# Loads moved to GpSimd's queue, and the conditions' rows read from memory, in a two-layer hybrid block

## The chip, the cores and the metric

The kernel runs on one core of a Trainium2 chip. The metric is the device time of one execution, in microseconds: before the change a median of 3194.43 us over three runs, from 3187.32 to 3200.40. The engines are named as in the profile: PE is TensorE (the matmuls), DVE VectorE, ACT ScalarE, POOL GpSimd, and SP SyncE, which only issues transfers. Each engine works through its own queue of instructions in order. ScalarE and GpSimd issue transfers too, and such an instruction stands in their queue like any other.

## What is computed

Two layers work on 1024 latent tokens `x` and 256 context tokens, each of width 1024. Every layer scales and shifts its normed input by six vectors that come from a condition, adds a mixer's output, and then an MLP's with a squared ReLU.

```python
mod_l = (silu(c) @ ada_w[l] + ada_b[l]).reshape(b, 6, 1, D)      # latent tokens
mod_c = (silu(c_ctx) @ ada_w[l] + ada_b[l]).reshape(6, D)        # context tokens
h_l = modulate(rmsnorm(x, norm1_g[l]), mod_l[:, 0], mod_l[:, 1])
x = x + mod_l[:, 2] * mixer(h_c, h_l)      # layer 0: attention and retention, layer 1: state space
h_l = modulate(rmsnorm(x, norm2_g[l]), mod_l[:, 3], mod_l[:, 4])
x = x + mod_l[:, 5] * (square(relu(h_l @ w1)) @ w2)
```

The context tokens take the same path in layer 0 with `mod_c`. The mixer of layer 1 (`s5_mixer`) runs a complex linear recurrence for 64 groups of 16 channels in both directions, and a gated output, `za * sigmoid(zb)` with `gelu(y) @ w_glu`, follows it.

## The kernel before

Tokens lie along the free axis in three blocks, 0 and 1 of 512 latent tokens and 2 of 256 context tokens; channels lie on the 128 partitions, eight tiles deep. Products in float32 are made of three matmuls (`mm3`, lines 68 to 72) from a high and a low part of each operand: L70 and L71 take the high weights, L72 the low ones, and the parts are made by `hi` (L76, mostly on ScalarE) and `lo` (L84, VectorE or GpSimd). Weights come through `split` (L1004): SP loads 512 KB into `mraw`, three buffers deep, ScalarE makes `uh` (or `dh`), VectorE `ul` (or `dl`).

The stages in order are: the first modulations, attention and retention, the output product, the first MLP in two passes (blocks 0 and 2 together, from about 1074 us, and block 1 alone, from about 1635 us), the state-space mixer (about 2085 to 2268 us), the gated output (to about 2475 us) and the second MLP.

In an MLP the hidden blocks go in pairs: a pair's first product is put through the ReLU and squared on ScalarE (`r`, L1053, `ah`, L1056), GpSimd makes its low part (`al`, L84), and the second product of the pair is added to `x` by VectorE (L1070), which frees the bank for TensorE.

Beside the first MLP side work is drawn in pieces, at a fixed rate for each matmul. It is, in order: the condition rows (`ada_row`), the modulation vectors of layer 1 (`ada_rest` with `aw` loads and a VectorE product-and-sum, L216), the tables of the state-space mixer, its input coefficients (`s5_inputs`, which loads `wb` and `ww`, L1347 and L1350, multiplies them to `wo` on VectorE, L1365 to L1369, and stores them as `bst` from ScalarE's queue), more tables (`tq`, `ta`), and the mixer's input for blocks 0 and 2 (`s5_in`, which stores `us` to `ud` in memory, L1454). Block 1's input follows after the MLP.

`ada_row` (L198 to L200) loads the condition to all partitions as `silr` from GpSimd's queue, and ScalarE puts the Silu on it. It is called at the start, ahead of the first MLP, and at the end of the state-space mixer, there for the last three modulation vectors, whose 96 `aw` loads of 128 KB are drawn during the gated output.

The mixer's loop takes 32 pairs of groups: `spread` negates and copies the oscillation table `CS` on ScalarE, `states` builds the decay `dec` on ScalarE, makes the inputs on TensorE (L1501), multiplies and scans them on VectorE (`st`, `sm`, `sz`), and makes `sy` on VectorE or GpSimd; `outs` brings these to the outputs on TensorE (L1536).

The framework orders each engine's instructions itself when the program is built, by its own estimate of when each could run. So the order in the queues is not that of the source: a change in one place can move instructions elsewhere, and one in the source may move none. [...] The pool of tiles from which `aw`, `wb`, `ww`, `wo` and others of 512 columns come (`atile`) has 32 buffers, and the one of 256 columns 16.

Of the kernel before, what the change touches and what calls it, by code (L numbers as in the profile page):

```python
# [18 lines left out]
P = 128  # L19
# [32 lines left out]
class Net:  # L52
# [93 lines left out]
    def ada_start(self, p, wk):  # L146

        nc, I = self.nc, self.I
        ct = p.tile([P, KT, 2], F32, name="ct")
        nc.sync.dma_start(ct, I["cT"])  # L150
        nc.scalar.activation(self.sc, ct, AF.Silu)
        cs = []
        for k in range(2):
            c = wk.tile([P, 512], F32R, tag="t5", name="cs").rearrange("p (k n) -> p k n", n=P)
            ks = slice(4 * k, 4 * k + 4)
            nc.vector.tensor_scalar(c, self.ones.unsqueeze(1).to_broadcast([P, 4, P]), 0.0, None, ALU.mult)
            nc.vector.tensor_copy(c[:, :, 0:2], self.sc[:, ks])
            nc.vector.tensor_tensor(c[:, :, 2:4], self.sc[:, ks], c[:, :, 0:2].bitcast(F32), ALU.subtract)
            cs += [c[:, j] for j in range(4)]
        return cs  # L160
# [31 lines left out]
    def ada_row(self, tile, ns=2, n=512):  # L192

        r = []
        for s in range(ns):
            for k in range(1024 // n):
                t = tile(f"silr{s}{k}")
                self.nc.gpsimd.dma_start(  # L198
                    t, self.I["crow"][s, n * k:n * k + n].unsqueeze(0).to_broadcast([P, n]))
                self.nc.scalar.activation(t, t, AF.Silu)  # L200
                r.append(t)
        return r

    def ada_rest(self, tile, rows, todo, n=512):
        nc, I = self.nc, self.I
        nk = 1024 // n
        for l, j in todo:
            ns = 2 if (l == 0 or j < 2) else 1
            for kt in range(KT):
                for k in range(nk):  # L210
                    w = tile()
                    nc.sync.dma_start(w, I["adat"][l, j, kt, :, n * k:n * k + n])
                    for s in range(ns):
                        m = self.M[:, l, j, kt, s:s + 1]
                        o = w if s == ns - 1 else tile()
                        nc.vector.tensor_tensor_reduce(o, w, rows[nk * s + k], 1.0,  # L216
                                                       m if k else self.bias[:, l, j, kt:kt + 1],
                                                       ALU.mult, ALU.add, m)
                    if ns == 2 or k == nk - 1:
                        yield  # L220
# [1118 lines left out]
    def s5_inputs(self):  # L1339
# [4 lines left out]
        def fetch(d, g0):  # L1344
            b, w = ([self.atile(name=nm) for _ in range(2)] for nm in ("wb", "ww"))
            for r in range(2):
                nc.sync.dma_start(b[r], bass.AP(  # L1347
                    tensor=I["s5bt"].tensor, offset=I["s5bt"].offset + (d * 2 + r) * 4096 + g0 * 64,
                    ap=[[0, 8], [16384, 16], [1, 512]]))
                nc.sync.dma_start(w[r], bass.AP(  # L1350
                    tensor=self.pbd.tensor, offset=self.pbd.offset + (d * 16 + r) * 4096 + g0 * 64,
                    ap=[[8192, 8], [0, 16], [1, 512]]))
# [89 lines left out]
    def s5_in(self, bi, x, tmp, b=None):  # L1442
# [5 lines left out]
        def o(kt, u, sh):  # L1448
# [4 lines left out]
            for c0 in ((32 + t0 // 8,) if t0 < NL else (0, 160)):  # L1453
                nc.sync.dma_start(rows[:, :, c0:c0 + nchunk], us.rearrange("p (s c) -> p s c", s=8))  # L1454
        return self.norm(1, 0, 1 if t0 >= NL else 0, lambda kt: x[:, kt, t0:t0 + n], n, o, tmp, b)

    def s5_main(self, p, last):
# [9 lines left out]
        self.Y = {(kt, th): self.atile(name="y") for kt in range(KT) for th in range(2)}  # L1467
        sl, A, ybank = {}, {}, {}

# [13 lines left out]
        def spread(q):  # L1483

            CS = sl[q][3]
            nc.scalar.activation(CS[:, :, 0], CS[:, :, 3], AF.Copy, scale=-1.0)
            nc.scalar.activation(CS[:, :, 1], CS[:, :, 2], AF.Copy)

        def states(q):

            B, C, Tt, CS = sl[q]
            dec = p.tile([P, 2, 2, 160], F32, tag="dec", name="dec", bufs=2)
            for d in range(2):
                nc.scalar.activation(dec[:, d], mask, AF.Copy, scale=self.R8[:, 2 * q + d:2 * q + d + 1])
            t = p.tile([P, 2, 2, 320], F32, tag="st", name="st", bufs=1)
# [56 lines left out]
        inputs(0, 8, (nc.scalar, nc.sync))  # L1552
        self.drain(last)
        for q in range(32):
            spread(q)
            states(q)
            if q % 4 == 0 and q < 28:
                inputs(2 * q + 8, 8)
# [46 lines left out]
    def run(self, stop=None):  # L1605
# [108 lines left out]
        def side():  # L1714
            rows = self.ada_row(lambda name: self.atile(name=name))
            yield
            yield from self.ada_rest(lambda: self.atile(name="aw"), rows, [(1, j) for j in range(3)])
            self.s5_setup(gp)
# [23 lines left out]
        with ExitStack() as st:  # L1742
# [20 lines left out]
            def mods():  # L1763
                yield from self.ada_rest(a256, self.ada_row(a256, 1, 256), [(1, 4), (1, 3), (1, 5)], 256)
            mods = mods()
# [37 lines left out]
def prepare(i):  # L1803
# [6 lines left out]
    o["adat"] = g["ada_w"].reshape(2, 1024, 6, 8, 128).transpose(0, 2, 3, 4, 1)  # L1810
    o["crow"] = np.stack([g["c"][0], g["c_ctx"]])
    o["adab"] = g["ada_b"].reshape(2, 6, 8, 128).transpose(3, 0, 1, 2)
# [49 lines left out]
```

## Time and profile before

| what | value |
|---|---|
| median of three runs | 3194.43 us |
| profiled execution, its own time | 3195.87 us |
| its span, first to last instruction | 3193.8 us |
| TensorE's mean granted clock in it | 0.967 of full speed |
| transfers | 324.26 MB, mean 102 GB/s |
| from SP's and GpSimd's queue, `aw` | 112 of 256 KB and 96 of 128 KB, all on SP |
| `silr` from GpSimd's queue | 8 of 256 KB and 4 of 128 KB |

The profile is of one execution. A stretch of it is read from the busy time of each engine in it and from the waits, which name what ended an idle time; the instruction that ends a wait is the last of several when there are several. The granted clock is the share of full speed at which TensorE was let run.

### The profile page before, as it was taken

Reading aid. Unit: us, or ns where it says so; the run is one execution under the profiler, and the core shown is the slowest. Engines: PE = TensorE matmul, PEld = TensorE weight load, DVE = VectorE, ACT = ScalarE, POOL = GpSimd, SP = SyncE. Lnnn points to the kernel's source line nnn. Section 1 sums busy time; section 2 is a strip of 40 time slices with the busy share of each in tenths; the row PEclk is TensorE's granted clock in tenths of the full one; section 3 lists DMA queues with packets and bytes.
Section 4 is the critical chain, followed back from the end, with each engine's and each line's share of the span. In section 5 each row is a group of like instructions: output and inputs, shape, how many; then the busy total and the mean of one; then the engine's idle time right before and its main releaser. Section 6 shows DMA issues by size and latency. Waiting matters only on the chain. (4 is left out here: it accounts for less than half of the span.)

```text
span 3193.8 us, 45085 instructions
## 1 busy us (share of the span) xinstructions
PE 2964.4 (93%) x16683; PEld 2441.1 (76%) x16683; DVE 2137.4 (67%) x4088; ACT 1255.4 (39%) x2559; POOL 732.7 (23%) x702
## 2 busy tenths in 40 slices
PE   5899998899999999999998898968899999999998
PEld 3777777688878788888886686757678788888887
DVE  6777777687764588366676697478855555556555
ACT  6542332666662322322342266344434322222221
POOL 3642222455450111111110010123222111111111
PEclk8999999999999999999999999989999999999999
DMA  7132222211011352233336755488642111111111
GB/s 252 70 119 81 78 79 66 82 29 26 13 59 61 114 178 75 66 107 91 104 112 214 219 174 152 139 188 223 217 128 93 53 43 50 53 47 51 42 47 66
DMA packets 259036, 324.26 MB, mean 102 GB/s; under 512 B 72336, under 2 KB 179632, under 8 KB 258816
## 3 DMA queue, kind: packets, MB, share of 16 engines
q1 hardware_dynamic: 197776, 280.63, 29.2%
q10 hardware_dynamic: 59840, 37.24, 3.8%
q0 software_dynamic: 1200, 3.51, 0.4%
q8 instruction: 131, 2.15, 0.3%
q14 instruction: 89, 0.73, 0.1%
HBM read 267.96 MB, written 53.35 MB: 101 GB/s over the span
## 5 line engine op out<-in xcount | busy, mean ns | idle before, releaser
L84 POOL TENSOR_TENSOR al<-r,ah 128x512 fp32r<-128x512 f32 (+1 forms) x160 | 210.2, 1325 | 1468.1 <-ACT r L1057 1344.1
L1070 DVE SCALAR_TENSOR_TENSOR x<-b,mods,x 128x512 f32<-128x512 f32 (+1 forms) x483 | 460.5, 965 | 105.2 <-PE b L72 99.9
L84 DVE TENSOR_TENSOR ul<-mraw,uh 128x512 fp32r<-128x512 f32 x256 | 194.7, 767 | 394.6 <-ACT uh L76 394.2
L70 PE MATMUL b<-ah,dh 128*128 128x512 f32 (+1 forms) x1088 | 412.5, 379 | 1.6 <-DVE u L264 1.4
L71 PE MATMUL b<-al,dh 128*128 128x512 f32 (+1 forms) x1088 | 411.2, 378 | 0.7 <-POOL al L84 0.7
L72 PE MATMUL b<-ah,dl 128*128 128x512 f32 (+1 forms) x1088 | 410.2, 378 | 0.0
L76 ACT ACTIVATE uh<-mraw 128x512 fp32r<-128x512 f32 x256 | 160.1, 628 | 473.0 <-PE b L71 261.2
L70 PE MATMUL b<-h2h,uh 128*128 128x512 f32 (+1 forms) x768 | 284.8, 371 | 42.8 <-DVE x L1070 30.0
L72 PE MATMUL b<-h2h,ul 128*128 128x512 f32 (+1 forms) x768 | 280.5, 366 | 5.4 <-DVE ul L84 5.4
L71 PE MATMUL b<-h2l,uh 128*128 128x512 f32 (+1 forms) x768 | 280.5, 365 | 0.0
L70 PEld LDWEIGHTS b<-ah,dh 128*128 128x128 f32 x1088 | 205.3, 189 | 41.3 <-issue 2.3
L71 PEld LDWEIGHTS b<-al,dh 128*128 128x128 f32 x1088 | 205.3, 189 | 38.1 <-POOL al L84 1.1
L72 PEld LDWEIGHTS b<-ah,dl 128*128 128x128 f32 x1088 | 205.2, 189 | 38.3
L70 PEld LDWEIGHTS b<-h2h,uh 128*128 128x128 f32 x768 | 148.6, 193 | 72.7 <-DVE x L1070 33.4
L76 ACT ACTIVATE dh<-mraw 128x512 fp32r<-128x512 f32 x192 | 116.4, 625 | 221.2 <-PE b L71 102.0
L70 PE MATMUL b<-h3h,uh 128*128 128x512 f32 x512 | 202.2, 395 | 0.0
L71 PE MATMUL b<-h3l,uh 128*128 128x512 f32 x512 | 199.9, 391 | 2.0 <-DVE h3l L313 1.7
L72 PE MATMUL b<-h3h,ul 128*128 128x512 f32 x512 | 201.0, 393 | 0.0
L84 POOL TENSOR_TENSOR pl<-pe,ph 128x512 fp32r<-128x512 f32 (+1 forms) x128 | 158.4, 1246 | 154.9 <-ACT ph L76 87.0
L1053 ACT ACTIVATE r<-b 128x512 f32<-128x512 f32 (+1 forms) x160 | 88.0, 551 | 252.0 <-PE b L72 188.8
L72 PEld LDWEIGHTS b<-h2h,ul 128*128 128x128 f32 x768 | 148.5, 193 | 32.5 <-DVE ul L84 7.7
L70 PE MATMUL z<-wh,hh 128*128 128x512 f32 (+1 forms) x400 | 161.6, 404 | 11.8 <-ACT scr L497 6.2
(422 smaller groups left out, 7036.2 us busy)
## 6 DMA issues: line engine op xcount, KB each, us to landing
mraw<-in_w SPq DMA_DIRECT2D x192, 512.0 KB
aw<-in_adat SPq DMA_DIRECT2D x112, 256.0 KB
mraw<-in_glu SPq DMA_DIRECT2D x32, 512.0 KB
aw<-in_adat SPq DMA_DIRECT2D x96, 128.0 KB
CS<-csd SPq DMA_DIRECT2D x32, 320.0 KB
w<-in_adaw SPq DMA_DIRECT2D x32, 256.0 KB
wraw<-in_winr SPq DMA_DIRECT2D x32, 256.0 KB
cst<-oc ACTq DMA_DIRECT2D x64, 128.0 KB
```

What stands on the lines that cost most here:

```text
L70: mm(o, s[0], m[0], start=start, stop=False)
L71: mm(o, s[0], m[1], start=False, stop=False)
L72: mm(o, s[1], m[0], start=False, stop=stop)
L76: self.nc.scalar.activation(o, x, AF.Copy)
L84: e.tensor_tensor(o, x, h.bitcast(F32), ALU.subtract)
L1053: nc.scalar.activation(r[:, :n], b[:, :n], AF.Relu)
L1070: nc.vector.scalar_tensor_tensor(o, as_x(b), self.M[:, l, 5, oc, s:s + 1], xs, op0=ALU.mult, op1=ALU.add)
```

## The change

There are five parts.

1. The Silu of both conditions is made once, as it was already for the first modulations, and now also written to memory (`scd`, two transfers from GpSimd's queue). `ada_row` loads its rows from there and applies no Silu any more: twelve activations of ScalarE go, and four table loads with them. The input `crow` is no longer needed.
2. The `aw` loads of layer 1 go from SP's queue to GpSimd's: 48 of 256 KB beside the first MLP, 96 of 128 KB at the gated output. Those of layer 0 stay.
3. The 64 loads of `wb` and `ww`, 256 KB each, go from SP's queue to GpSimd's.
4. The `ud` stores of blocks 0 and 2 go to GpSimd's queue, 8 and 16 of them, each of 1024 short runs (256 or 128 bytes). Block 1's eight stay on SP.
5. In the mixer's loop `spread` of a pair, with `dec` in it now, is called a pair ahead, after `states` of the pair before.

```diff
         nc.scalar.activation(self.sc, ct, AF.Silu)
+        self.scd = self.dram.tile([2, 1024], F32, name="scd")
+        for s in range(2):
+            nc.gpsimd.dma_start(self.scd[s].rearrange("(k p) -> p k", p=P), self.sc[:, :, s])
         cs = []
             c = wk.tile([P, 512], F32R, tag="t5", name="cs").rearrange("p (k n) -> p k n", n=P)
...
                 self.nc.gpsimd.dma_start(
-                    t, self.I["crow"][s, n * k:n * k + n].unsqueeze(0).to_broadcast([P, n]))
-                self.nc.scalar.activation(t, t, AF.Silu)
+                    t, self.scd[s, n * k:n * k + n].unsqueeze(0).to_broadcast([P, n]))
                 r.append(t)
-    def ada_rest(self, tile, rows, todo, n=512):
+    def ada_rest(self, tile, rows, todo, n=512, eng=None):
         nc, I = self.nc, self.I
+        eng = eng or nc.sync
         nk = 1024 // n
                     w = tile()
-                    nc.sync.dma_start(w, I["adat"][l, j, kt, :, n * k:n * k + n])
+                    eng.dma_start(w, I["adat"][l, j, kt, :, n * k:n * k + n])
                     for s in range(ns):
                         o = w if s == ns - 1 else tile()
...
             for r in range(2):
-                nc.sync.dma_start(b[r], bass.AP(
+                nc.gpsimd.dma_start(b[r], bass.AP(
                     tensor=I["s5bt"].tensor, offset=I["s5bt"].offset + (d * 2 + r) * 4096 + g0 * 64,
                     ap=[[0, 8], [16384, 16], [1, 512]]))
-                nc.sync.dma_start(w[r], bass.AP(
+                nc.gpsimd.dma_start(w[r], bass.AP(
                     tensor=self.pbd.tensor, offset=self.pbd.offset + (d * 16 + r) * 4096 + g0 * 64,
             return b, w
...
             for c0 in ((32 + t0 // 8,) if t0 < NL else (0, 160)):
-                nc.sync.dma_start(rows[:, :, c0:c0 + nchunk], us.rearrange("p (s c) -> p s c", s=8))
+                (nc.sync if bi == 1 else nc.gpsimd).dma_start(rows[:, :, c0:c0 + nchunk], us.rearrange("p (s c) -> p s c", s=8))
         return self.norm(1, 0, 1 if t0 >= NL else 0, lambda kt: x[:, kt, t0:t0 + n], n, o, tmp, b)
     def s5_main(self, p, last):
...
         self.Y = {(kt, th): self.atile(name="y") for kt in range(KT) for th in range(2)}
-        sl, A, ybank = {}, {}, {}
+        sl, A, ybank, decs = {}, {}, {}, {}
             B, C = (self.atile(name=nm).rearrange("p (d w k) -> p d w k", d=2, w=2) for nm in "BC")
...
             nc.scalar.activation(CS[:, :, 1], CS[:, :, 2], AF.Copy)
-
-        def states(q):
-
-            B, C, Tt, CS = sl[q]
             dec = p.tile([P, 2, 2, 160], F32, tag="dec", name="dec", bufs=2)
                 nc.scalar.activation(dec[:, d], mask, AF.Copy, scale=self.R8[:, 2 * q + d:2 * q + d + 1])
+            decs[q] = dec
+
+        def states(q):
+
+            B, C, Tt, CS = sl[q]
+            dec = decs.pop(q)
             t = p.tile([P, 2, 2, 320], F32, tag="st", name="st", bufs=1)
                 vb = self.bank()
...
         self.drain(last)
+        spread(0)
         for q in range(32):
-            spread(q)
             states(q)
+            if q < 31:
+                spread(q + 1)
             if q % 4 == 0 and q < 28:
             if q < 29:
...
             yield
-            yield from self.ada_rest(lambda: self.atile(name="aw"), rows, [(1, j) for j in range(3)])
+            yield from self.ada_rest(lambda: self.atile(name="aw"), rows, [(1, j) for j in range(3)], eng=nc.gpsimd)
             self.s5_setup(gp)
             for bi in (0, 2):
...
             def mods():
-                yield from self.ada_rest(a256, self.ada_row(a256, 1, 256), [(1, 4), (1, 3), (1, 5)], 256)
+                yield from self.ada_rest(a256, self.ada_row(a256, 1, 256), [(1, 4), (1, 3), (1, 5)], 256, nc.gpsimd)
             mods = mods()
             self.drain(mods)
...
     o["adat"] = g["ada_w"].reshape(2, 1024, 6, 8, 128).transpose(0, 2, 3, 4, 1)
-    o["crow"] = np.stack([g["c"][0], g["c_ctx"]])
     o["adab"] = g["ada_b"].reshape(2, 6, 8, 128).transpose(3, 0, 1, 2)
     w = g["w_in"][0]
```

What this makes of the order shows at three places. The first is the second pass of the first MLP. SP's queue near the end of the coefficient loads, before; `mraw` are the MLP's weights:

```order
L1004 DMA mraw<-in_w 128x1024 x2
L1347 DMA wb<-in_s5bt 128x1x512
L1350 DMA ww<-pbd 128x1x512
L1347 DMA wb<-in_s5bt 128x1x512
L1350 DMA ww<-pbd 128x1x512
L1004 DMA mraw<-in_w 128x1024 x23
L1454 DMA ud<-us 1024x1x64 x8
L1004 DMA mraw<-in_w 128x1024
```

SP's queue over the whole pass, after, with the loads of the mixer's `T` tables behind it:

```order
L1286 DMA pbd<-pbs 128x4x128
L1007 DMA mraw<-in_w 128x1024 x2
L1286 DMA pbd<-pbs 128x4x128
L1007 DMA mraw<-in_w 128x1024 x79
L1481 DMA T<-tst 128x1x128 x4
L1007 DMA mraw<-in_w 128x1024 x3
L1481 DMA T<-tst 128x1x128 x4
```

GpSimd's queue where the coefficient loads begin, after; `al` is the low part of a hidden block:

```order
L84 TENSOR_TENSOR al<-r,ah 128x256 x2
L1350 DMA wb<-in_s5bt 128x1x512
L84 TENSOR_TENSOR al<-r,ah 128x512
L1353 DMA ww<-pbd 128x1x512
L1350 DMA wb<-in_s5bt 128x1x512
L1353 DMA ww<-pbd 128x1x512
L84 TENSOR_TENSOR al<-r,ah 128x512
```

The loads of `wb` and `ww` no longer stand between the `mraw`, 79 of which now follow each other on SP; they stand between the `al` on GpSimd, from one to nine in a row. Later in that pass GpSimd's queue has the `ud` stores, after:

```order
L84 TENSOR_TENSOR al<-r,ah 128x512 x12
L1457 DMA ud<-us 1024x1x64 x6
L84 TENSOR_TENSOR al<-r,ah 128x512
L1457 DMA ud<-us 1024x1x64 x2
L84 TENSOR_TENSOR al<-r,ah 128x512
L1457 DMA ud<-us 1024x1x32 x16
L84 TENSOR_TENSOR al<-r,ah 128x512 x6
```

They stood on SP, eight and sixteen in two rows between `mraw`, and now stand between the last `al` of the pass.

The second place is the mixer's loop on ScalarE. Before, with the outputs `y` of four pairs:

```order
L1487 ACTIVATE CS<-CS 128x2x160
L1494 ACTIVATE dec<-mask,R_12294 128x320 x6
L1486 ACTIVATE CS<-CS 128x2x160
L1487 ACTIVATE CS<-CS 128x2x160
L1541 ACT_TABLE_LOAD
L1541 ACTIVATE y<-z 128x4x4x16
```

The same place after:

```order
L1490 ACTIVATE CS<-CS 128x2x160
L1493 ACTIVATE dec<-mask,R_12289 128x320 x6
L1489 ACTIVATE CS<-CS 128x2x160
L1490 ACTIVATE CS<-CS 128x2x160
L1546 ACT_TABLE_LOAD
L1546 ACTIVATE y<-z 128x4x4x16
```

Nothing moved but the line numbers; the same holds for the whole loop on this engine, and for TensorE, VectorE, GpSimd and SP in it.

The third place is the end of the mixer and the start of the gated output. SP's queue before, behind the last pair's tables:

```order
L1475 DMA C<-cst 128x512
L1478 DMA T<-tst 128x1x128 x2
L212 DMA aw<-in_adat 128x256 x27
L1004 DMA mraw<-in_glu 128x1024 x3
L212 DMA aw<-in_adat 128x256 x7
L1004 DMA mraw<-in_glu 128x1024
```

GpSimd's queue after; on SP all 32 `mraw` of the gated output now follow each other directly behind the tables:

```order
L1523 TENSOR_TENSOR sy<-sz,CS 128x512
L1523 TENSOR_TENSOR sy<-sz,CS 128x4x128
L215 DMA aw<-in_adat 128x256 x11
L1523 TENSOR_TENSOR sy<-sz,CS 128x4x128
L215 DMA aw<-in_adat 128x256 x6
L1523 TENSOR_TENSOR sy<-sz,CS 128x512
L215 DMA aw<-in_adat 128x256 x42
L1601 TENSOR_TENSOR x<-x,sgm 128x4x128
```

The `aw` loads left SP, where 27 stood ahead of the first `mraw`, and stand between and behind the last `sy` on GpSimd. On VectorE 33 of their products now stand ahead of the first `yl`, the low part of the gated output's operand; it was 27. `x` in the last row is the residual sum of the gated output.

## The prediction

> **What bounds the kernel now.** I read the page first, for the share of each engine, then the table of stretches, the waits of TensorE, the waits of the other engines inside the worst stretch, and last the timeline at three places where the change acts.
>
> ```profile
> span 3193.8 us, 45085 instructions
> PE 2964.4 (93%) x16683; PEld 2441.1 (76%) x16683; DVE 2137.4 (67%) x4088; ACT 1255.4 (39%) x2559; POOL 732.7 (23%) x702
> ```
>
> TensorE works 2964.4 of 3193.8 us. The change removes no matmul, so all it can win lies in the 229.4 us in which TensorE stands idle, and in the clock that it is granted. The next table has a stretch to a row: its length, the busy time of each engine, then TensorE's granted clock, the busy share of the DMA engines and GB/s.
>
> ```profile
> 0.00:54.00 54.00, 31.69 (x103) 17.05 (x104) 33.54 (x86) 34.67 (x61) 10.97 (x20) 0.95 0.96 316
> 1350.00:1690.00 340.00, 334.07 (x2260) 285.93 (x2258) 230.81 (x435) 111.04 (x230) 45.23 (x35) 0.99 0.36 108
> 1678.00:1850.00 172.00, 143.76 (x583) 114.89 (x582) 118.33 (x195) 52.11 (x89) 17.45 (x13) 0.91 0.70 212
> 1690.00:1694.00 4.00, 2.19 (x5) 1.81 (x6) 3.60 (x6) 2.44 (x5) 0.00 (x0) 0.60 0.52 192
> 1848.80:1895.40 46.60, 46.60 (x204) 37.95 (x204) 46.11 (x116) 29.96 (x53) 5.59 (x5) 1.00 0.59 181
> 1850.00:2052.00 202.00, 185.46 (x781) 148.72 (x780) 148.13 (x336) 114.36 (x198) 20.43 (x16) 0.96 0.57 160
> 2093.00:2268.00 175.00, 140.89 (x2690) 120.04 (x2687) 151.54 (x181) 67.72 (x154) 61.06 (x46) 0.89 0.83 211
> 2268.00:2475.00 207.00, 192.61 (x868) 155.86 (x867) 127.86 (x279) 85.38 (x131) 48.25 (x28) 0.98 0.44 140
> ```
>
> TensorE's waits over the whole span follow: who waited for whom, the sum, the number of times, the longest.
>
> ```profile
> PE b L70 <- DVE x L1070: 30.3, 8, 7.5
> PE z L1536 <- DVE sy L1518: 16.5, 5, 5.0
> PE b L279 <- ACT sq L277: 14.4, 1, 14.4
> PE b L70 <- ACT uh L76: 14.3, 6, 5.9
> ...
> PE b L1575 <- ACT y L1541: 7.6, 1, 7.6
> ```
>
> The stretch from 1678 to 1850 is the second pass of the first MLP while the coefficient operands (`wb`, `ww`) are loaded and multiplied beside it: 172.0 − 143.76 = 28.2 us idle. Inside it the same view gives, for TensorE, VectorE and ScalarE in turn:
>
> ```profile
> PE b L70 <- DVE x L1070: 28.2, 5, 7.5
> ```
> ```profile
> DVE ul L84 <- ACT uh L76: 30.9, 11, 6.7
> DVE wo L1367 <- DMA ww<-pbd: 10.2, 4, 3.1
> DVE wo L1365 <- DMA ww<-pbd: 4.5, 2, 2.9
> ```
> ```profile
> ACT uh L76 <- DMA mraw<-in_w: 35.6, 6, 11.8
> ACT dh L76 <- DVE wo L1369: 15.1, 4, 5.1
> ```
>
> TensorE waits for VectorE's `x` (a bank to be emptied), `x` stands in VectorE's queue behind `ul`, `ul` waits for ScalarE's `uh`, and `uh` for the weight load `mraw`, up to 11.8 us. `mraw` stands on SP's queue among 64 loads of `wb` and `ww`. That is the largest single thing that the change touches.
>
> **The change part by part.**
>
> *Coefficient operands.* With `wb` and `ww` on GpSimd, SP has nothing but `mraw` there. A pair of hidden blocks that does not stall takes 23.3 us (46.60 us without idle time for two, the row from 1848.80). The stretch from 1678.0 to 1848.8 holds six: 170.8 − 6 × 23.3 = 31.0 us of excess, of which 28.2 is idle time and the rest the clock (0.91 against 0.99 to 1.00 beside it). What could keep some of it: VectorE waits for `ww` itself, 14.7 us, and that wait does not vanish with the queue. While mostly `wb` and `ww` move (1690 to 1694), the DMA engines are 0.52 busy at 192 GB/s, where the start reaches 0.96 at 316: such loads seem to keep only half of the engines busy, an inference, as the trace does not tell engines apart. If so the busy half was nearly full in this stretch (0.70 on average), and `mraw`, which uses all, was slow by it. Bounds: nothing gained if `ww` remains the last to come, 31.0 gained if all goes. I take 24, nearer to the upper end, since the path to TensorE ends in `mraw` and not in `ww`.
>
> [...]
>
> *Mixer inputs `ud`.* 24 of 32 stores go from SP to GpSimd. The rows are the stores' durations on SP (minimum, median, maximum in ns), three issues on GpSimd (start, duration), and TensorE's group that waits for `al`.
>
> ```profile
> L1454 SPq DMA_DIRECT2D ud<-us x32: 513/658/1972, 1966.3 to 2093.7; - x32
> ```
> ```profile
> 3.02 2.12 POOL L198 DMA_DIRECT2D silr<-in_crow  x4
> ...
> 5.65 0.50 POOL L346 DMA_DIRECT2D rn<-in_iota  x1
> 6.14 0.57 POOL L401 DMA_DIRECT2D cosr<-in_cosR  x1
> ```
> ```profile
> L71 PE MATMUL b<-al,dh 128*128 128x512 f32 (+1 forms) x1088 | 411.2, 378 | 0.7 <-POOL al L84 0.7
> ```
>
> On SP one cost 0.66 us (median, at most 1.97) to issue, ahead of `mraw`. From 1850 to 2052 TensorE idles 16.5 us; I take 5 of it as gained, with 0 and 14 as ends (14.3 us is all that it waited for `uh` anywhere). On GpSimd an issue takes 0.50 (8 rows) to 0.57 us (128 rows). A `ud` store has 1024 runs; the trace has none like it on GpSimd. By the small slope between those two rows it costs about 1 us, by eight times the row of 128 about 4.5. The slope is the nearer comparison, so I take 1 us: 24 us over the stretch, hidden under `al`'s lead, which I estimate at one pair of blocks, 23 us, since a pair's `al` is used while the next is made (TensorE waited 0.7 us for `al` in all).
>
> *Modulation weights, first MLP.* 48 loads go to GpSimd: 48 × 0.55 = 26 us of issue where GpSimd is busy 45.23 of 340 us (the row from 1350). SP's longest wait from 1115 to 1600 is for VectorE, which frees the buffers of `mraw`:
>
> ```profile
> SPq L1004 <- DVE dl L84: 232.5, 27, 16.5
> ```
>
> SP has time to spare there. Gain and cost nothing; if GpSimd had no time to spare, 26 us would be the price.
>
> *The conditions' rows.* The Silu goes at three places, its table loads with it. The rows are from the timeline (start, duration, and in brackets the idle time before and what ended it); the last is the time from issue to landing of all twelve `silr` loads.
>
> ```profile
> 10.90 0.63 ACT L200 ACTIVATE silr<-silr 128x512 f32<-128x512 f32 x1 [7.24 <-DMA silr<-in_crow]
> ...
> 13.72 4.25 ACT L277 ACTIVATE sq<-hx 128x512 f32<-128x512 f32 x8
> ```
> ```profile
> 1064.25 2.23 POOL L198 DMA_DIRECT2D silr<-in_crow  x4 [103.94 <-PE b L72]
> ...
> 1068.04 1.28 ACT L200 ACT_TABLE_LOAD   x1 [3.84 <-DMA silr<-in_crow]
> ...
> 1070.00 0.75 DVE L216 CUSTOM_DVE_ANT_0 aw<-aw,silr,adab 128x512 f32<-128x512 f32 x1 [6.10 <-ACT silr L200]
> ```
> ```profile
> DMA to landing us min/median/max: 3.7/5.4/9.6
> ```
>
> At the start ScalarE's first square is held until 13.72 by Silus that wait for their loads, and TensorE until 14.4. The DMA engines are 0.96 busy there, so a square that starts earlier soon meets loads that have not landed, and later work of the start needs the same bytes. Gain 0 to 2.8 (13.72 − 10.90, what three Silus and the gaps between them take); I take 2. Before the first MLP the Silus go, but the first modulation product now waits for its weight on GpSimd, issued after four `silr` at about 1066.5 and landing, by 3.7 to 9.6 us, at 1070 to 1076 instead of ready at 1070.0. `x` moves ahead of it in the new order, the later `h2l` and `ul` stay behind it. TensorE's stall there was 5.9 us; I take a gain of 2, from 5 gained to 3 lost.
>
> *Phases a pair ahead.* In the loop of the state-space mixer the order of ScalarE is the same before and after: `dec` and `CS` stand where they stood, and so do the rows of the other engines. The scheduler had already placed them so. I cost it at nothing, both ways; the 16.5 us for `sy` stay in the forecast.
>
> *End of the mixer, gated output.* 96 loads leave SP, where 27 stood in a row ahead of the first `mraw`. Timeline rows of SP, ScalarE, TensorE, VectorE and GpSimd there:
>
> ```profile
> 2269.53 1.32 SPq L1004 DMA_DIRECT2D mraw<-in_glu  x3
> ```
> ```profile
> 2274.58 0.63 ACT L76 ACTIVATE uh<-mraw 128x512 fp32r<-128x512 f32 x1 [17.97 <-issue]
> 2275.23 1.28 ACT L1541 ACT_TABLE_LOAD   x1
> ```
> ```profile
> 2277.79 3.53 PE L1575 MATMUL b<-ident,y 128*128 128x128 f32 x12 [7.56 <-ACT y L1541]
> 2281.40 0.50 PE L70 MATMUL b<-yh,uh 128*128 128x512 f32 x1
> ```
> ```profile
> 2272.83 0.49 DVE L216 CUSTOM_DVE_ANT_0 aw<-aw,silr,mods 128x256 f32<-128x256 f32 x1
> ```
> ```profile
> 2262.99 1.29 POOL L1518 TENSOR_TENSOR sy<-sz,CS 128x512 f32<-128x512 f32 x1 [6.35 <-DVE sz L1512]
> ```
>
> `mraw`, `uh` and the table load no longer hold `y`; the 7.56 us before the transposes go. What is late next is VectorE's `yl`: 33 modulation products stand ahead of it (27 before), and their loads now come from GpSimd, the last sixteen of them behind the `sy` that ended at 2264.3. The 33rd leaves at 2264.3 + 16 × 0.55 = 2273, lands 3.7 to 5.4 us later, and `yl` comes 0.5 us after that: 2277 to 2279. The first product at 2281.40 then comes 2 to 4 us sooner, and with the longest landing (9.6 us) 2 us later. I take 3.
>
> The sum: 24 + 5 + 0 + 2 + 2 + 0 + 3 = 36 us. The profiled run took 3195.87 us, 2.1 beyond its span, 1.4 above the median of 3194.43. 3195.87 − 36 = 3160.
>
> **The rivals.**
>
> *The loads, not the queue.* `ww` on GpSimd lands no sooner, VectorE keeps waiting (14.7 us) and ScalarE behind `wo` with it. Then of the 24 nothing comes, and the rest gives 12: 3184 (3177 to 3192). For it: the rows of `wo`. Against it: `mraw`, 35.6 us, is longer than they are.
>
> *GpSimd's queue jams: slower.* In the new order up to nine loads stand between two `al`, twelve to a pair of blocks. Each waits for a buffer that VectorE frees and for the landing of an earlier one. If a load takes t, a pair of blocks takes 12 t, which decides from 23.3 / 12 = 1.94 us on. At 3 us each of 64 / 12 = 5.3 pairs lasts 12.7 us more than the unstalled one: +68 instead of −31 of the excess. 3195.87 + 68 − 31 − 12 = 3221. For it: landings of 3.7 to 9.6 us. Against it: several are in flight at a time, and four `silr` issued 2.23 us in all.
>
> *Stores with short runs hold GpSimd: slower.* At 4.5 us a `ud`, sixteen in a row hold the next `al` for 72 us against a lead of 23: +49, less the other gains of 31: 3214. It decides from 23.3 / 16 = 1.5 us on. For it: nothing in the trace has 1024 runs on that queue. Against it: 8 rows and 128 rows cost 0.50 and 0.57. [...]
>
> *All of it.* The excess of 31 goes, with 14 from the second half and the 7 of the other places: 3195.87 − 31 − 14 − 7 = 3144, and at the neighbours' clock in the second half (0.99 for 0.96, of 185 us) 6 less, 3138.
>
> **How the numbers follow.** Forecast (3140 to 3177): 0.55. Loads, not the queue: 0.20, about a third of it faster by more than 0.5%. Jam: 0.09. Short runs: 0.06. All of it: 0.10. A measurement of this kernel can tell 0.5%, 16 us, from no change, so faster ends at 3178.5 and slower begins at 3210.4. Faster: 0.55 + 0.10 + 0.07 = 0.72; same: 0.13; slower: 0.15. The range runs from 3132, where in the case of all the start, the first MLP and the gated output give their upper ends too (2.8 + 5 + 4 for 7), to 3200, where in the case of the loads they and the second half give their lower ends (0, −3, −2 and 0 for 12, 3201); the two slower cases are left out.
>
> **What would show it.** Right: SP's weight loads in the second pass follow one another, TensorE's wait for `x` at L1070 falls from 30.3 to under 8 us, a pair of blocks takes 23 to 24 us, the mixer's waits for `sy` are as before, and transposes begin near 2271 less what was won before. Wrong: TensorE waits for `al`, GpSimd's stores take over 1.5 us each, VectorE's `wo` waits more for `ww` than 14.7 us, or the gated output starts later than before.

## The result and the profile after

| | before | after |
|---|---|---|
| median | 3197.41 us (4 runs, 3187.32 to 3201.14) | 3171.14 us (4 runs, 3169.79 to 3179.58) |
| ratio after to before | | 0.9932, 95% interval 0.9905 to 0.9959 |
| profiled execution | 3195.87 us | 3179.58 us, the longest of its four runs |

The kernel became 0.7% faster: 26 us by the medians, 22 by the ratio. The forecast was 3160 us, in a range from 3132 to 3200. The page of after, against the two lines shown of before:

```profile
span 3177.8 us, 45251 instructions
PE 2964.2 (93%) x16683; PEld 2445.6 (77%) x16683; DVE 2142.5 (67%) x4088; ACT 1247.1 (39%) x2543; POOL 866.5 (27%) x936
```

TensorE has the same 2964 us of work; GpSimd has 234 more instructions, the loads and stores that it took over. The waits of TensorE:

```profile
PE b L70 <- DVE x L1073: 22.9, 12, 5.9
PE z L1541 <- DVE sy L1523: 15.1, 4, 5.2
PE b L1506 <- DMA ut<-ud: 13.8, 1, 13.8
PE b L176 <- ACT wh L76: 12.4, 5, 8.4
...
PE b L1582 <- DVE yl L84: 9.4, 1, 9.4
...
PE b L70 <- ACT uh L76: 7.0, 4, 3.2
...
PE b L282 <- ACT sq L280: 6.0, 1, 6.0
```

Three things are to be seen. The wait for `x` fell, but from 30.3 to 22.9 us and not to under 8. The first square now holds TensorE 6.0 us in place of 14.4, but a wait of 12.4 us for `wh`, the weights of the first modulations, has come in. And the wait of 7.6 us for `y` ahead of the gated output is now one of 9.4 us for `yl`.

For the second pass of the first MLP I cut both traces at the same matmuls: the six pairs of hidden blocks beside which the coefficient operands are loaded, and the rest of the pass. Before, then after (length, busy time of TensorE, its weight loads, VectorE, ScalarE, GpSimd, then granted clock, share of the DMA engines, GB/s):

```profile
1692.00:1857.00 165.00, 142.40 (x576) 114.08 (x577) 119.60 (x204) 54.68 (x94) 16.22 (x12) 0.91 0.69 208
1857.00:2050.00 193.00, 176.46 (x741) 141.32 (x740) 141.20 (x320) 108.86 (x188) 20.37 (x15) 0.96 0.58 162
```
```profile
1700.00:1853.00 153.00, 140.05 (x577) 112.01 (x577) 131.37 (x231) 59.78 (x102) 45.95 (x61) 0.96 0.89 232
1853.00:2032.00 179.00, 172.74 (x742) 139.59 (x743) 133.93 (x291) 104.41 (x181) 41.35 (x39) 0.98 0.59 169
```

The six pairs became 12 us shorter and the rest 14. VectorE has 27 more instructions in the first stretch and 29 fewer in the second, though none was added: with the loads on another queue, the scheduler put work that belongs to the mixer's tables (`ta` and `tq`, range reductions for sines) earlier among the `x` of VectorE. Ahead of the 212th such `x` of the kernel VectorE had done 1 of the 236 instructions of that work, now it has done 25. The prediction had not looked for that. Idle time of TensorE went from 22.6 to 13.0 us in the first stretch and from 16.5 to 6.3 in the second.

**How far a single trace can be read.** The profiled run of after spent 416.75 us in attention, that of before 408.19. No instruction is moved there. Over all the kernels below the same stage took either 408 to 409 or 415 to 419 us, with each part of the change present or absent. So the total of one run says little below some 9 us, and I compare stages, between the first matmuls of each, over all traces that have a part against all that lack it. A stage is read from one profiled execution of each kernel, and the number of traces stands beside each mean.

### The profile page after: what moved, and what is told of

The parts are those of the page before. It is cut to its first block, busy times and chain, and to the rows that moved or that the text cites. A ratio compares the mean times of both kernels' runs of the same rounds, so it can differ in the third digit from the quotient of the medians.

```text
span 3177.8 us, 45251 instructions
## 1 busy us (share of the span) xinstructions
PE 2964.2 (93%) x16683; PEld 2445.6 (77%) x16683; DVE 2142.5 (67%) x4088; ACT 1247.1 (39%) x2543; POOL 866.5 (27%) x936
## 2 busy tenths in 40 slices
DMA packets 223774, 324.32 MB, mean 102 GB/s; under 512 B 52432, under 2 KB 147440, under 8 KB 223552
```

## The experiments

My theory after the result: two places of the change gave time back (the write of the conditions' rows at the start, the modulation weights ahead of the gated output), and the gain of the coefficient operands is smaller than 24 us because their loads, from GpSimd's queue, fill the DMA engines (0.89 busy in the six pairs, for 0.69 before). The rivals: the difference is the spread of runs; the row of `wb` that eight groups of partitions read at once is slow; the parts work otherwise when they are alone.

### Each part alone

**The conditions' rows alone**, on the kernel before:

```
+        self.scd = self.dram.tile([2, 1024], F32, name="scd")
+        for s in range(2):
+            nc.gpsimd.dma_start(self.scd[s].rearrange("(k p) -> p k", p=P), self.sc[:, :, s])
...
-                    t, self.I["crow"][s, n * k:n * k + n]...)
-                self.nc.scalar.activation(t, t, AF.Silu)
+                    t, self.scd[s, n * k:n * k + n]...)
```

> Before with part 1 alone (rows from memory, no Silu). Theory: the write of scd in 2048 pieces of 4 bytes holds the DMA engines from 12 to 24 us, so the first square comes early (first matmul at 6 us for 14.4) and yet the first product of the low parts, the matmul z<-wh,hh, begins at about 56 us for 53.4. If the write costs nothing, that product begins at 51 us or earlier. Before the first MLP the modulation weights are still on SP here, so the first matmul on h2h comes 4 to 6 us after the output product's last (7.2 before, 3.95 with all parts): nearer to 2 if the Silu was all that held it, near 4 if it was not.

Measured: 3191.92 us. From the span's start to the first product with `hh` it took 56.44 us; before it was 53.40. Ahead of the first MLP the stall stayed at 7.2 us, above the 4 to 6 expected. The rows cost time at the start, and alone they win nothing at the MLP, since the first modulation product then waits for its weight (6.7 us, where it waited 6.1 us for the Silu before).

**The coefficient operands alone**:

```
-                nc.sync.dma_start(b[r], bass.AP(
+                nc.gpsimd.dma_start(b[r], bass.AP(
-                nc.sync.dma_start(w[r], bass.AP(
+                nc.gpsimd.dma_start(w[r], bass.AP(
```

> Before with part 3 alone (wb and ww on GpSimd). Theory: this alone gives the 12 us of the first six pairs of blocks in the second pass (165 us from the 545th to the 641st h2h matmul before, 153 with all parts), and DMA share there is 0.9 to 1.0 with about 190 GB/s where only these loads move. Of the 14.5 us of the second half it gives little, under 4, if the ud stores on SP are their cause; it gives 10 or more if that half was late because of the order that the loads left behind.

Measured: 3174.61 us, 31 below the one run of before beside it; six pairs 145.57 us (165.20 before), the rest of the pass 183.39 (193.34 before). So the rest gave 10 us without the `ud` stores having moved, which speaks for the order that the loads leave behind. This one run was a short one, as ten more of the same kernel show further down.

**The stores of `ud` alone**:

```
-                nc.sync.dma_start(rows[:, :, c0:c0 + nchunk], us...)
+                (nc.sync if bi == 1 else nc.gpsimd).dma_start(rows[:, :, c0:c0 + nchunk], us...)
```

> Before with part 4 alone (the ud stores of blocks 0 and 2 on GpSimd). Theory: 10 to 14 us less in the second half (193 us from the 641st h2h matmul to the last one before, 179 with all parts), as ScalarE's uh no longer waits for mraw behind 24 stores. Rival, the order left by the coefficient loads: under 4 us. A ud store takes 0.9 to 2.3 us on GpSimd in either case.

Measured: 3189.23 us; six pairs 162.85, the rest 187.76 against 193.34 before: 5.6 us, where the prediction had 5. It lies between the 10 to 14 of the theory and the under 4 of its rival.

**The modulation weights alone**:

```
-                    nc.sync.dma_start(w, I["adat"][l, j, kt, :, n * k:n * k + n])
+                    eng.dma_start(w, I["adat"][l, j, kt, :, n * k:n * k + n])
```

> Before with part 2 alone (modulation weights of layer 1 on GpSimd). Theory: nothing within 2 us in the first pass of the MLP, and the gated output's first product comes 16 to 18 us after the mixer's last matmul (13.6 before, 16.7 with all parts), since VectorE waits for weights that land late behind the gated output's own loads. Rival, the rows from memory cause it: 13 to 14 us, no change.

Measured: 3215.24 us, but 11 us of what it lies above before are in attention (419.39), and 8 in the stage behind the start (495.39), where nothing is moved. The stages that the part touches: 5.57 us ahead of the first MLP (7.21 before), 16.86 us from the mixer's end to the first product of the gated output (13.80 before). It wins nothing.

### Parts of after undone

**The conditions' rows written later.** The Silus stay away from the start, but the two writes wait for the first modulations:

```
-        for s in range(2):
-            nc.gpsimd.dma_start(self.scd[s].rearrange("(k p) -> p k", p=P), self.sc[:, :, s])
...
         self.gains(0, 0)
+        nc.vector.scalar_tensor_tensor(self.sc2, self.M[:, 0, 0], 0.0, self.sc, op0=ALU.mult, op1=ALU.add)
+        for s in range(2):
+            nc.gpsimd.dma_start(self.scd[s].rearrange("(k p) -> p k", p=P), self.sc2[:, :, s])
```

> After, with scd written only once the first modulations are done (a copy that depends on them is written). Theory (the 4-byte writes hold the DMA engines during the start): the matmul z<-wh,hh begins at 47 to 51 us for 56.1, 5 to 9 us gained there, and nothing else changes. Rival (the start is bound by the bytes of its weights, whatever is written): 53 to 56 us.

Measured: 3156.21 us; the start took 44.49 us, less than the 47 to 51 expected, against 56.10 of after and 53.40 of before. What the write did is seen in the DMA engines from 9 to 21 us. Before, then after:

```profile
DMA packets 2395, 4.04 MB, mean 337 GB/s; under 512 B 361, under 2 KB 1137, under 8 KB 2395
```
```profile
DMA  9999999999999999990310103679399999846497
GB/s 362 382 396 389 335 369 396 369 376 369 369 326 273 260 213 101 43 20 17 31 20 7 7 10 68 82 85 51 44 96 120 171 99 102 106 99 123 68 68 61
DMA packets 1569, 2.07 MB, mean 172 GB/s; under 512 B 248, under 2 KB 1016, under 8 KB 1569
...
scd<-silc POOLq DMA_DIRECT2D x2, 4.0 KB, 11.4
```

By its access pattern each write moves 4 KB as 1024 separate numbers of 4 bytes, and the two take 11.4 us (median) to land. Meanwhile half of the bytes move that moved before. The same stretch of the start, by its clock, in after and in the kernel with the late write:

```profile
12.00:16.00 4.00, 2.78 (x7) 0.95 (x6) 3.11 (x17) 3.04 (x4) 0.00 (x0) 1.00 1.98 127
16.00:20.00 4.00, 0.00 (x0) 0.00 (x0) 2.89 (x1) 0.00 (x0) 0.00 (x0) 0.95 0.89 91
20.00:24.00 4.00, 0.77 (x1) 0.29 (x1) 0.69 (x1) 0.63 (x1) 2.19 (x4) 0.50 0.78 128
```
```profile
12.00:16.00 4.00, 2.73 (x7) 0.94 (x5) 2.39 (x13) 3.21 (x5) 0.00 (x0) 1.00 1.04 343
16.00:20.00 4.00, 1.56 (x4) 0.70 (x4) 4.00 (x4) 2.57 (x5) 0.00 (x0) 0.96 0.95 301
20.00:24.00 4.00, 4.00 (x13) 3.24 (x12) 4.00 (x7) 3.69 (x6) 0.00 (x0) 0.62 1.05 395
```

From 16 to 20 us after has not one matmul; its weights `w` are on the way at 91 GB/s. (A packet's time is counted whole where the packet starts, so a share can lie above 1.) The packets of the loads beside the write took long: between 12 and 24 us 44 of them took over 1 us, the longest 5.4 us, and in the kernel with the late write one did. There such packets come from 44 us on, beside the write, up to 3.5 us. So it is shown that the writes hold up the loads beside them.

What they cost is not the whole difference of the two starts, for the `silr` loads wait for the write and leave the start with it, 1 MB in four transfers. After, then the kernel with the late write:

```profile
20.16 1.13 POOL L201 DMA_DIRECT2D silr<-scd  x2 [9.51 <-DMA scd<-silc]
```
```profile
54.08 0.59 POOL L203 DMA_DIRECT2D silr<-scd  x1 [6.43 <-DMA scd<-sc]
```

From 12 to 24 us 2.8 MB less moved than in the kernel with the late write (1.38 against 4.15). At the 339 GB/s of its start that is 8 us, and the 1 MB of `silr` is 3 us; both are estimates, and no kernel separates the two.

**The gated output's modulation weights back on SP**, all else as after:

```
-    ... [(1, 4), (1, 3), (1, 5)], 256, nc.gpsimd)
+    ... [(1, 4), (1, 3), (1, 5)], 256)
```

> After, with the gated output's 96 weight loads back on SP. Theory (their landing on GpSimd behind the 32 loads of mraw delays VectorE's yl): the gated output's first product comes 11 to 14 us after the mixer's last matmul for 16.7. Rival (yl is late because 33 products stand ahead of it, wherever their loads are issued): 16 to 17 us.

Measured: 3173.56 us; from the mixer's end to the gated output 13.82 us, where after has 16.89. TensorE's waits there, first after, then this kernel:

```profile
PE b L1582 <- DVE yl L84: 9.4, 1, 9.4
```
```profile
PE b L1582 <- ACT y L1546: 6.9, 1, 6.9
```

And what VectorE, which makes `yl`, waits for there in after:

```profile
DVE aw L219 <- DMA aw<-in_adat: 8.5, 2, 4.3
DVE ul L84 <- ACT uh L76: 2.2, 2, 1.8
```

In after `y` came early, as forecast, and `yl` then was last: it stands behind products whose weights had not landed. This holds in all fourteen traces: `yl` is last in the seven with these weights on GpSimd, `y` in the seven with them on SP. But the edit also put VectorE's order back, with 28 products ahead of the first `yl` for the 33 of after (33 to 35 in the seven, 27 or 28 in the others). So the rival, the number of products, is not separated from their landing. Nor is the size far above the spread: with these weights on SP the row took 13.8 to 16.3 us (mean 14.9 of seven traces), with them on GpSimd 15.4 to 17.5 (mean 16.1 of seven).

**`wb` from rows of its own.** The operand lies eight times in memory, so that no two partitions read the same row:

```
-                    ap=[[0, 8], [16384, 16], [1, 512]]))
+                    ap=[[16384, 128], [1, 512]]))
```

> After, with wb read from an input that holds its 16 rows eight times, so that each partition reads a row of its own; bytes, tiles and queue are the same. Theory (many partitions reading the same row of memory is what keeps these loads at 190 GB/s, their packets of 4096 bytes at 260 to 330 ns for 159): wb lands in 4 to 6 us for 8.1, DMA share from 1680 to 1853 falls from 0.91 to 0.75 to 0.8, and the first six pairs of blocks take 4 to 10 us less than 153. Rival (loads from GpSimd's queue are slow by themselves): packets, share and 153 us stay within 2 us.

Measured: 3159.47 us; `wb` landed in 6.7 us (median) in place of 8.1, where 4 to 6 were expected; the six pairs took 145.35 us, with the DMA engines 0.84 busy for 0.89. With the shared rows the same order of instructions took 145.6 to 161.3 us in six traces. So the result is at the lower end of what happens without this edit: not settled.

### Are the DMA engines the limit in the second pass?

**Half of each load.**

```
-                nc.gpsimd.dma_start(b[r], bass.AP(
+                nc.gpsimd.dma_start(b[r][:, 0:256], bass.AP(
-                    ap=[[0, 8], [16384, 16], [1, 512]]))
+                    ap=[[0, 8], [16384, 16], [1, 256]]))
...
-                nc.vector.tensor_tensor(x, w[0], b[r], ALU.mult)
+                nc.vector.tensor_tensor(hv(x), hb(w[0]), hb(b[r]), ALU.mult)
```

(`ww` and the second product likewise; `hb` reads the first half twice.)

> The kernel after, but each load of wb and ww brings only the first 256 of its 512 columns, and the products use these twice: half of the coefficients is left out, the count of issues and of vector instructions is unchanged. Theory (the bytes of these loads fill the DMA engines, 0.87 to 0.91 busy in the first six pairs): the wait of TensorE for x falls from 10 to 20 us to under 3, the six pairs take 139 to 144 us (147 to 161 in three runs of the same order), the run comes to 3160 to 3165. Rival (GpSimd's queue, its issues and its waits for buffers): nothing changes, six pairs 147 to 161, the run 3170 to 3180.

Measured: 3163.0 us; the six pairs 147.04 us: longer than the 139 to 144 of the theory, at the very lower end of the rival's 147 to 161. The run lies in the 3160 to 3165 of the theory, and TensorE's wait for `x`, 11.5 us, does not (under 3 expected). The six pairs and the rest in this kernel:

```profile
1693.50:1840.50 147.00, 135.80 (x576) 108.77 (x576) 138.96 (x259) 63.32 (x110) 49.37 (x56) 0.99 0.72 203
1840.50:2016.00 175.50, 171.07 (x742) 138.21 (x743) 124.42 (x261) 99.67 (x172) 41.87 (x39) 0.99 0.57 165
```

The DMA engines' share fell from 0.89 to 0.72, and TensorE still idled 11.2 us. But VectorE is now 138.96 of 147.00 us busy, with 259 instructions where after has 231: the scheduler, which knew the smaller loads, drew still more of the later work forward. So the edit changed two things, and it can't price the bytes alone. Two things are left standing. Full engines are not the whole limit, since it remains when they have room. And in after they are part of what keeps `mraw` late, as ScalarE's waits in the six pairs show, first after, then half the loads:

```profile
ACT uh L76 <- DMA mraw<-in_w: 31.2, 7, 6.8
ACT dh L76 <- DVE wo L1372: 15.3, 4, 5.2
```
```profile
ACT dh L76 <- DVE wo L1374: 22.7, 8, 3.8
ACT uh L76 <- DMA mraw<-in_w: 16.1, 5, 4.2
```

With half the bytes `mraw` holds ScalarE half as long, and VectorE's `wo` takes the first place. My theory that full DMA engines alone bound this stage falls.

### The coefficient operands, timed, and the best version

**Only this part undone in after** (`wb` and `ww` back on SP, the diff of the part alone turned round):

> The kernel after with wb and ww back on SP, all else as after. Theory (this part is worth about 21 us: 11 in the first six pairs, 10 in the rest of the pass): 3190 to 3194. The prediction's term (24) gives 3195. Rival (what TensorE wins in the first six pairs is only the spread of runs, and the part is worth 10 or less): 3178 to 3181.

Measured: median 3195.29 us of 10 runs (3190.82 to 3202.92), ratio to before 0.999, 0.9975 to 1.0004. Without the coefficient operands the change is worth nothing that can be measured, and with them 24 us more by the medians, which is the prediction's term.

**Only this part done**, the kernel of the second experiment above:

> The kernel before with wb and ww on GpSimd, nothing else: the same part alone, timed. Theory (21 us): 3172 to 3178, ratio 0.992 to 0.995. By the single look that it had (31 below the run beside it): 3164 to 3168. Rival (10 or less): 3185 to 3190.

Measured: median 3179.41 us of 10 runs (3162.0 to 3197.82), ratio 0.9936, 0.9911 to 0.9961: 18 us by the medians, 20 by the ratio. The median falls in neither range of numbers, between the theory and the rival, nearer to the theory. The runs of this kernel differ by 36 us, those of the one above by 12, and the nineteen of before by 21; why they differ so much is not shown.

**The best version**: late write, the last modulation weights on SP, `wb` from its own rows.

> The kernel after with the conditions' rows written to memory only after the first modulations, the last modulation weights on SP, and wb from rows of its own. Theory (the writes of single numbers cost about 10 us at the start, the others 0 to 3): 3156 to 3160, 11 to 15 us under the kernel after, ratio to before 0.987 to 0.989. Rival (the start's gain is given back later, by the clock or by loads that come later): 3166 to 3171.

Measured: median 3151.1 us of 4 runs (3147.55 to 3159.02), ratio to before 0.9845, 0.9816 to 0.9875. It beats both kernels, 20 us under after, and came out 5 us under what the theory gave. The start took 47.00 us; the six pairs:

```profile
1678.00:1823.00 145.00, 136.05 (x577) 109.02 (x578) 132.52 (x231) 60.04 (x103) 47.82 (x58) 0.99 0.85 245
```

**Of these only the late write**, timed:

> The kernel after with only the write of the conditions' rows moved behind the first modulations, now timed. If the first writes cost the 9 to 12 us of the start's rows and nothing else differs: 3159 to 3162 (median after 3171). If the other two edits of the best kernel (wb from rows of its own, the last modulation weights on SP) are worth nothing, this kernel stands level with it: 3148 to 3154. If wb's own rows are worth what the first six pairs show (152 us without, 145 with them), it stays 7 to 9 us above it, 3158 to 3160.

Measured: median 3163.06 us of 4 runs (3155.4 to 3166.57), ratio 0.9887, 0.9857 to 0.9916; the start 46.08 us. It is 8 us under after by the medians, 1 above the range of 3159 to 3162, so not all of the start's 11 us is seen in the total. The stage behind the start, in which the late write now runs, took 489.3 us (mean of three) against 486.8 with the early write (six), inside its spread of 483.7 to 495.4. The median lies 12 above the best version, as if the other two edits were worth something; but the intervals of the two ratios overlap (0.9857 to 0.9916, 0.9816 to 0.9875), and I leave that open.

## Why the prediction was nearly right

By stages, means over the traces with and without a part (the number of traces in brackets; traces with half loads or own rows of `wb` are left out of the second pass):

| term | forecast gain | without | with | measured gain |
|---|---|---|---|---|
| coefficient operands: two pairs where the loads begin | (in 24) | 40.1 (5) | 38.5 (6) | 1.6 |
| the next six pairs | 24 | 163.6 (5) | 151.1 (6) | 12.5 |
| rest of the pass, without `ud` | 0 | 192.6 (3) | 183.3 (2) | 9.3 |
| `ud`, rest of the pass | 5 | 192.6 (3) | 187.8 (2) | 4.8 |
| conditions' rows, start | 2 | 53.9 (5) | 56.9 (6) | −3.0 |
| rows and weights, first MLP's start and first pass | 2 | 581.4 (4) | 580.7 (8) | 0.6 |
| phases a pair ahead, mixer | 0 | 174.9 (6) | 174.1 (8) | 0.8 |
| gated output's start | 3 | 14.9 (7) | 16.1 (7) | −1.3 |
| sum | 36 | | | 25.3 |

The sum of 25.3 us agrees with the timed 22 to 26. The 11 us that separate it from 36 are those by which the forecast of 3160 missed 3171.14: 5 at the start, 4 at the gated output, the rest at the first MLP.

**Coefficient operands: the size was met, by another path than the one forecast.** The step "SP has nothing but `mraw` there" holds; but for 3.6 us SP waited for VectorE alone. SP's waits in the six pairs of after:

```profile
SPq L1007 <- DVE dl L84: 89.9, 11, 13.8
SPq L1007 <- DVE ul L84: 43.3, 11, 9.0
SPq L1007 <- DVE ta L1327: 12.5, 2, 7.3
SPq L1007 <- DMA mraw<-in_w: 3.6, 2, 2.3
```

The step that failed is "since the path to TensorE ends in `mraw` and not in `ww`". With the queue free, ScalarE waited no less for `mraw`. In the six pairs `uh` waited 31.2 us for it in after (the row above), and before, cut at the same matmuls, 26.3 us; the 35.6 us of the prediction are from a longer cut. What VectorE waited for `uh` fell all the same. Before, then after:

```profile
ACT uh L76 <- DMA mraw<-in_w: 26.3, 6, 5.5
```
```profile
DVE ul L84 <- ACT uh L76: 25.8, 10, 6.7
```
```profile
DVE ul L84 <- ACT uh L76: 10.1, 5, 3.4
```

Over the five traces with these loads on SP and the six with them on GpSimd (those of the table above), the means of the waits in the six pairs are:

| wait | on SP | on GpSimd |
|---|---|---|
| ScalarE for `mraw` | 25.2 us | 32.9 us |
| ScalarE for `wo`, whose stores `bst` it issues | 52.0 | 27.3 |
| VectorE for `ww` | 10.7 | 1.0 |
| VectorE for `uh` | 27.6 | 11.8 |
| TensorE for `x` | 24.0 | 14.2 |

So the gain came along `ww` and `wo`, the path that the prediction had left to its rival, and not along `mraw`. How much of it is due to the loads and how much to VectorE's new order is not separated. A pair of hidden blocks took 25.2 us (151.1 / 6), not the 23 to 24 forecast.

From GpSimd's queue the loads of `wb` and `ww` fill the DMA engines, and there they meet `mraw`, for which ScalarE waits 32.9 us in place of 25.2: while nearly only these loads move, queue by queue,

```profile
DMA packets 689, 1.15 MB, mean 191 GB/s; under 512 B 351, under 2 KB 421, under 8 KB 689
## 3 DMA queue, kind: packets, MB, share of 16 engines
q0 software_dynamic: 608, 1.10, 100.7%
```

(from 1684 to 1690 us of after), their packets alone take 100.7% of the engines' time, at 191 GB/s in all. On SP, from 1690 to 1694 us of before, the engines were 0.52 busy at 192 GB/s. That only half of them were in use there stays an inference: the traces give the share, and not which engines. The packets took 324 ns for 4096 bytes from GpSimd's queue (median), and 84 ns for 2048 bytes from SP's. The full 31 us, the prediction's upper bound, did not come: the six pairs gave 12.5, and the rate of such loads did not rise. What made up for it is a term that the prediction did not have, 9.3 us in the rest of the pass; that the sum meets 24 is luck. Timed alone and undone, the part is worth 18 to 24 us against a forecast of 24. In the rest of the pass none of these loads is issued any more, before or after (the last at 1818.5 and 1803.3 us). That the reordering of VectorE is the cause of the 9.3 is what the counts suggest (141.20 to 133.93 us of VectorE there, and the same counts in the kernel with this part alone); a kernel with the old order and the new queue was not tried.

**`ud`: right.** 5.6 us in the kernel with this part alone. The stores on GpSimd:

```profile
L1457 POOL DMA_DIRECT2D ud<-us x24: 847/1228/2262, 1951.6 to 1983.7; - x24
```

A store of 1024 runs took 1.23 us in the median against the 1 us taken by the slope and far from 4.5. So the rival of the short runs falls. VectorE was busy for 19.87 of the 34.40 us from 1951.6 to 1986.0, in which they were issued, and no store took over 2.3 us. TensorE waited 0.7 us for `al`, as before.

**Conditions' rows at the start: wrong twice.** The two writes were not costed at all, neither their issue nor what they do to the loads beside them; with the `silr` loads that leave with them they cost 11.0 us (56.9 − 45.9, the mean of the three starts with the late write), of which the writes alone are 8 by the estimate above. And the gain from the Silus' leaving was bounded at 2.8 us by their own time. Without the early write the start is 8.0 us shorter than before (53.9 − 45.9). The 1 MB of `silr` loads has left it, 3 us by the same estimate, and TensorE's wait for the first square falls from 14.4 us to this (kernel with the late write):

```profile
PE b L284 <- ACT sq L282: 5.8, 1, 5.8
```

The step "a square that starts earlier soon meets loads that have not landed" failed as a bound: 8.0 us came where it allowed 2.8. TensorE's idle time of 14.4 us was the wider bound, and not ScalarE's three Silus.

**First MLP: 2 forecast, 0.6 measured, inside the spread.** The stall itself fell from 7.21 to 3.95 us, and the first pass behind it became longer by 2.6.

**Phases: right.** The order is the same, and so is the time within the spread (172.8 to 176.8 with, 174.4 to 175.4 without).

**Gated output: wrong sign.** "`mraw`, `uh` and the table load no longer hold `y`" was right. What is late next was named too, `yl`, but its loads were costed as if they landed in 3.7 to 5.4 us after one issue each 0.55 us. In the trace of after GpSimd's queue stopped for the landing of earlier loads:

```profile
2248.85 3.71 POOL L215 DMA_DIRECT2D aw<-in_adat  x7 [0.34 <-PE b L1541]
2254.35 0.54 POOL L215 DMA_DIRECT2D aw<-in_adat  x1 [1.79 <-DMA aw<-in_adat]
2255.69 9.00 POOL L215 DMA_DIRECT2D aw<-in_adat  x17 [0.80 <-DMA aw<-in_adat]
```

**The rivals.** "The loads, not the queue" is refuted in its own row, from 1680 to 1853 us of after: `wo` waits for `ww` less than before. It was right that these waits were what counted.

```profile
DVE wo L1370 <- DMA bst<-wo: 8.8, 2, 5.0
DVE wo L1370 <- DMA ww<-pbd: 7.1, 3, 3.5
DVE wo L1368 <- DMA ww<-pbd: 0.5, 1, 0.5
```

7.6 us in all against 14.7 in the prediction's rows, and in the six pairs alone 1.9. A wait for the stores of the products (`bst`) now stands above it; it was 4.2 us before. GpSimd's queue did not jam, though its loads waited for VectorE and for landings in the six pairs, as SP's had waited for landings. SP before, then GpSimd after:

```profile
SPq L1347 <- DMA wb<-in_s5bt: 5.5, 4, 1.9
SPq L1004 <- DMA ww<-pbd: 4.7, 3, 3.0
```
```profile
POOL ww L1353 <- DMA bst<-wo: 21.9, 5, 9.2
POOL wb L1350 <- DMA bst<-wo: 5.4, 2, 4.4
POOL wb L1350 <- DVE wo L1370: 4.4, 2, 2.5
```

A load took 8 us to land, but one was issued every 3.1 us (49 in the 153 us of the six pairs), so that two or three were in flight, and TensorE did not wait for `al`. "All of it" fails with the 13.0 us in which TensorE still stands idle in the six pairs. (The lower end of the range comes out at 3133 by the prediction's own terms, 3138 − 4.8, and not at 3132.)

## What to carry to other kernels

Moving loads to a freer queue took away the order in which they stood, not the bytes (324.26 MB before, 324.32 after): ask whose waits it will shorten (here those for the moved loads, not those for the transfer that they stood among), what share of the DMA engines they will fill, and how the new queue reorders the other engines, since 9 of the 23 us here came from a stretch in which none of these loads is issued any more. Two stores of 4 KB in single numbers held the transfers beside them to 91 to 128 GB/s here (301 to 395 without them), so place such a store where no load is waited for. With stages that differ by some us from run to run (attention took 408 to 419 us), compare stages over several kernels, and don't price a part by the total of one run.

## What was not expected of the hardware

- Two writes of 4 KB, by their access pattern in pieces of 4 bytes, held the transfers of the start to 91 to 128 GB/s for 12 us (301 to 395 without them); the start was 11 us longer, of which an estimated 3 belong to the loads that wait for them.
- The same loads moved at about 190 GB/s with the DMA engines 0.52 busy from SP's queue and 1.0 busy from GpSimd's, in one short stretch of each: a larger share, no more bytes per second.
- Attention, where no instruction was moved, took 408 to 409 us in eight of the fourteen traces and 415 to 419 in the other six.
